# A hybrid decoder step: the beginning reordered, and column tiles in the modulation, the inverse and the sample z

## The chip, the core and the metric

The kernel runs as one program on one core of a Trainium2 chip. TensorE (matmuls, and beside them its weight loads), VectorE, ScalarE (ACT), GpSimd (POOL) and SyncE (SP, which issues the transfers) each work through their own instructions and wait for one another by semaphores. The metric is the time of one execution on the device in microseconds (us). All data are 32-bit floats. Most products split both operands into a high and a low part (`fp32r`) and add three products; the small ones are plain `f32` matmuls, which the profile shows as two instructions each.

## What is computed

One layer of a decoder: a modulated RMSNorm, one input projection, two groups of heads (a state-space one, SSD, and a gated delta rule, GDN), an output projection, a gate and a residual. It is applied to a prompt of 2048 rows and to 32 sample rows (8 sequences of 4). Cut to what matters here:

```python
mod = silu(c) @ w_ada + b_ada                     # c: 9 rows (1 prompt, 8 samples), w_ada: 1024 x 3072
shift, scale, gate = split(mod, 3)
h = rmsnorm(x, norm_w) * (1 + scale) + shift
proj = h @ w_in                                   # columns: z, conv inputs, gates of both head groups
xbc, _ = causal_conv4_silu(xbc_raw); qkv, _ = causal_conv4_silu(qkv_raw)
# GDN, per head and chunk:
A = strict_lower((beta * k) @ k.T * decay) + I
u, w = solve_triangular(A, [beta * v, beta * k * exp(gcum)])
# state passes from chunk to chunk; y = rmsnorm(o) * silu(z)
out = x + gate * (concat(ssd, gdn) @ w_out)
y = rmsnorm(out, final_norm_w)
```

## The kernel before

**Pieces.** The prompt is worked through in four pieces of 512 rows (`p` from 0 to 3). A piece holds its modulated rows transposed, as `hhi` and `hlo`: eight tiles k of 128 features by 512 rows. The last piece carries the 32 sample rows as 32 further columns. In a piece, the input projection runs through 104 half tiles of weights: a conv tile (128 output columns) has two halves of four k, twelve matmuls of 512 columns each; a z pair (256 output columns) has four quarters of two k. A half's weights come as 256 KB of floats into a buffer `xin` (three of them), and ACT and POOL split them into high and low (`want`, lines 495 and 496); some halves are stored split for later pieces. Four split halves can wait at once. Conv tiles add up in PSUM buffers of the tag `ip`, of which there are three; the smaller products use three of the tag `bk`. After its second half, a conv tile is evacuated by ACT and VectorE (`conv`, lines 536 to 549).

**Order.** TensorE's order is written out: each piece of work is entered with a time `tau` in units of about one conv half (`at(tau, f)`), and the work is issued by rising `tau`, 106 units to a piece. The order of the other engines and of SP's transfers is made by a planner that simulates the program; their waits follow from the data. `fill` enters weight halves into one list, by rising `tau`, so that `want` can load ahead.

**The beginning.** Ahead of the entered work, TensorE gets in this order: the first half of the shift (`ada_shift(0)`), the sums of squares of the first piece (`stat_first`), their spread over the partitions (`stat_row(0)`), the first half of the scale (`ada_scale(0)`). A half is 512 of the 1024 features. `ada_cols` makes 512 columns of the modulation: for each of eight k the nine columns of `sc` (silu of c) are the left side and 512 columns of `w_ada` are streamed past them (line 168), into nine rows of PSUM; ACT copies the nine rows (line 170), four transposes (line 173) turn them so that features are partitions, and VectorE adds the bias (line 174). The sums of squares use 32 matmuls with one streamed column each (line 300). `h_load` scales the x tiles by the row norm, `h_make` applies scale and shift and splits (lines 313 to 315). Only the first four k of `h` are made then; the other half (`second_half`) is entered at 2.3, after the first half of the first conv tile at 2. The gates (32 columns, `gates`) are made in five steps, entered at 0, 2.5, 4.1, 8.3 and 10.3: the product with the first four k, the product with the others, the turn (line 424) and the start of a chain on VectorE and ACT, the cumulative sum (lines 371 and 372), and the turn that is stored for the decays.

**The inverse.** For two heads at a time (a pair, 16 in the program) the eight 128 x 128 triangular matrices of a piece are inverted: blocks of 32 on VectorE, then `b2_1` to `b2_4` put the blocks together with matmuls. `b2_3` and `b2_4` (lines 852 to 864) are eight matmuls each, on 64 output rows and 64 streamed columns, evacuated in one copy each. Behind them come the `hop`s, which carry the state from chunk to chunk.

**Sample z.** In the last piece `z_pair` also makes z for the 32 sample rows: the rows are the left side (32 columns of `hhi` or `hlo`) and 256 columns of weights are streamed, three products per k (`zmm`, line 619).

**The gate columns** (`ada_gate`, line 195) are made among the last hops of the last piece, in two times four parts of two k, again with nine columns of `sc` on the left, and go to memory as rows. After that the pools are freed, and the output projection follows with the sample rows' heads among it.

## Time and profile before

| | |
|---|---|
| time, median of 3 runs | 2328.43 us (2324.95 to 2330.56) |
| profiled execution, its own time | 2327.78 us |
| its span in the profile | 2326.1 us |
| granted TensorE clock, mean | 0.979 |
| TensorE matmuls busy | 2200.8 us (95%) |
| TensorE weight loads busy | 1864.9 us (80%) |
| VectorE busy | 1481.9 us (64%) |
| ACT busy | 953.1 us (41%) |
| POOL busy | 826.7 us (36%) |
| read and written in memory | 289.89 MB, 95.30 MB |

A line such as `49.07 0.50 PE L414 MATMUL pbk<-hhi,wg 128*64 128x512 f32 x1 [3.98 <-ACT hhi L314]` is an instruction of TensorE (PE) at 49.07 us that took 0.50 us, made by line 414, which writes the PSUM tile `pbk` from `hhi` and `wg`: 128 rows by 64 columns of weights, 512 streamed columns; before it the engine was idle for 3.98 us until ACT had written `hhi`. "x8" puts eight like it together. PEld are weight loads, SPq is SyncE's issue of a transfer. Ends of matmuls are modelled, so that a start is a better mark than an end.

### The profile page before, as it was taken

Reading aid. Unit: us, or ns where it says so; the run is one execution under the profiler, and the core shown is the slowest. Engines: PE = TensorE matmul, PEld = TensorE weight load, DVE = VectorE, ACT = ScalarE, POOL = GpSimd, SP = SyncE. Lnnn points to the kernel's source line nnn. Section 1 sums busy time; section 2 is a strip of 40 time slices with the busy share of each in tenths; the row PEclk is TensorE's granted clock in tenths of the full one; section 3 lists DMA queues with packets and bytes.
Section 4 is the critical chain, followed back from the end, with each engine's and each line's share of the span. In section 5 each row is a group of like instructions: output and inputs, shape, how many; then the busy total and the mean of one; then the engine's idle time right before and its main releaser. Section 6 shows DMA issues by size and latency. Waiting matters only on the chain. (4 is left out here: it accounts for less than half of the span.)

```text
span 2326.1 us, 41856 instructions
## 1 busy us (share of the span) xinstructions
PE 2200.8 (95%) x15405; PEld 1864.9 (80%) x15405; DVE 1481.9 (64%) x3574; ACT 953.1 (41%) x2680; POOL 826.7 (36%) x1052
## 2 busy tenths in 40 slices
PE   6999999989999999999999989999999799998998
PEld 3688878868897887889788889998899377786786
DVE  2466868786767768675666776668676564454323
ACT  2534556454536445442533453435433432231111
POOL 3255665554437243411522241215211554322000
PEclk8999999999999999999999999999999999999999
DMA  6354655555766675465645544555445563643321
GB/s 239 113 167 152 191 166 180 181 181 174 225 214 209 213 225 183 143 193 165 191 153 179 178 135 132 180 154 157 150 147 160 165 211 125 191 155 128 129 86 52
DMA packets 241112, 387.94 MB, mean 167 GB/s; under 512 B 75880, under 2 KB 132968, under 8 KB 240908
## 3 DMA queue, kind: packets, MB, share of 16 engines
q1 hardware_dynamic: 240908, 385.28, 52.2%
q8 instruction: 121, 1.98, 0.3%
q14 instruction: 83, 0.68, 0.1%
HBM read 289.89 MB, written 95.30 MB: 166 GB/s over the span
## 5 line engine op out<-in xcount | busy, mean ns | idle before, releaser
L531 PE MATMUL pip<-hhi,w 128*128 128x512 f32 (+1 forms) x2880 | 823.7, 362 | 6.7 <-DVE kT L549 4.9
L531 PEld LDWEIGHTS pip<-hhi,w 128*128 128x128 f32 x2880 | 515.0, 190 | 85.0 <-issue 6.9
L531 PE MATMUL pip<-hlo,w 128*128 128x512 f32 (+1 forms) x1440 | 509.8, 354 | 0.0
L619 PE MATMUL pip<-w,hhi 128*128 128x256 f32 x2048 | 382.6, 287 | 0.3 <-DVE cv L549 0.3
L496 POOL TENSOR_TENSOR w<-xin,w 128x512 fp32r<-128x512 f32 x156 | 202.6, 1301 | 378.3 <-ACT w L495 344.8
L619 PEld LDWEIGHTS pip<-w,hhi 128*128 128x128 f32 x2048 | 316.5, 190 | 2.4 <-DVE cv L549 0.5
L531 PEld LDWEIGHTS pip<-hlo,w 128*128 128x128 f32 x1440 | 274.5, 191 | 36.9 <-issue 4.5
L619 PE MATMUL pip<-w,hlo 128*128 128x256 f32 x1024 | 289.4, 283 | 0.0
L1185 PE MATMUL pip<-wohi,mh 128*128 128x512 f32 x480 | 195.3, 407 | 7.4 <-ACT mh L1169 7.2
L619 PEld LDWEIGHTS pip<-w,hlo 128*128 128x128 f32 x1024 | 194.8, 190 | 0.0
L1185 PE MATMUL pip<-wohi,ml 128*128 128x512 f32 x480 | 189.7, 395 | 1.1 <-DVE ml L1176 1.0
L1185 PE MATMUL pip<-wolo,mh 128*128 128x512 f32 x480 | 189.1, 394 | 0.8 <-DVE wolo L238 0.8
L539 DVE SCALAR_TENSOR_TENSOR tr<-pip,cw,tr 128x509 f32<-128x509 f32 (+5 forms) x240 | 152.8, 637 | 40.2 <-ACT tr L536 37.1
L539 DVE SCALAR_TENSOR_TENSOR cv<-pip,cw,cv 128x509 f32<-128x509 f32 (+2 forms) x180 | 114.7, 637 | 44.6 <-ACT cv L536 42.5
L1000 POOL TENSOR_TENSOR L<-L,g_gc 128x512 f32<-128x512 f32 x64 | 70.9, 1120 | 198.4 <-DMA L<-rowsd 198.1
L495 ACT CAST w<-xin 128x512 fp32r<-128x512 f32 x156 | 95.1, 612 | 80.9 <-PE pip L619 25.9
L795 DVE TENSOR_TENSOR tl<-dl,ul 128x60 f32<-128x60 f32 (+21 forms) x432 | 121.0, 280 | 9.3
L797 DVE TENSOR_TENSOR dl<-dl,tl 128x60 f32<-128x60 f32 (+21 forms) x432 | 119.1, 276 | 9.0
L1185 PEld LDWEIGHTS pip<-wohi,mh 128*128 128x128 f32 x480 | 91.4, 190 | 27.0 <-ACT mh L1169 7.8
L1185 PEld LDWEIGHTS pip<-wohi,ml 128*128 128x128 f32 x480 | 91.0, 190 | 22.8 <-DVE ml L1176 3.0
L1185 PEld LDWEIGHTS pip<-wolo,mh 128*128 128x128 f32 x480 | 91.4, 190 | 18.2 <-DVE wolo L238 1.1
L1169 ACT CAST mh<-pch 128x512 fp32r<-128x512 f32 (+1 forms) x60 | 33.7, 562 | 166.4 <-PE pch L1166 166.3
(433 smaller groups left out, 4141.3 us busy)
## 6 DMA issues: line engine op xcount, KB each, us to landing
w<-wsp SPq DMA_DIRECT2D x260, 512.0 KB
wsp<-w SPq DMA_DIRECT2D x104, 512.0 KB
xin<-in_w_in SPq DMA_DIRECT2D x156, 256.0 KB
L<-rowsd SPq DMA_DIRECT2D x64, 256.0 KB
mx<-mixd SPq DMA_DIRECT2D x28, 512.0 KB
E<-rowsd SPq DMA_DIRECT2D x32, 256.0 KB
ul<-ud SPq DMA_DIRECT2D x64, 128.0 KB
mixd<-z SPq DMA_DIRECT2D x16, 512.0 KB
```

What stands on the lines that cost most here:

```text
L495: mark("ACT", s.copy(hi, rv))
L496: mark("POOL", g.tensor_tensor(lo, rv, hi, ALU.subtract))
L531: pe.matmul(pp, a[:, k, :], b[:, kk, cols], start=(i == 0), stop=(i == 23))
L539: v.scalar_tensor_tensor(u[:, c0 + dd:c0 + w], pp[:, 0:w - dd], cw[:, ci, k:k + 1], u[:, c0 + dd:c0 + w], ALU.mult, ALU.add)
L619: pe.matmul(out.rearrange("p (t c) -> p t c", t=2), a[:, k, cols], ws[b][:, :, k % 2, :], start=(first and k == 0 and e == 0), stop=(k == ...
L795: v.tensor_tensor(tmp[:, 0:r, 0:w], _bc(dl[:, 0:r, m], [P, r, w]), ul[:, m, m + 1:32].unsqueeze(1).to_broadcast([P, r, w]), ALU.mult)
L797: v.tensor_tensor(dl[:, 0:r, m + 1:32], dl[:, 0:r, m + 1:32], tmp[:, 0:r, 0:w], ALU.add)
L1000: g.tensor_tensor(L[:], L[:], _bc(G()["gc"][:, gi * 8 + q * 4:gi * 8 + q * 4 + 4, c], [P, 4, P]), ALU.subtract)
L1169: s.copy(mh[:, :, 0:n], ptv)
L1185: pe.matmul(pos[hb][0:m, :], a[:, k, 0:m], b[q * 4 + k][:, hb * 512:(hb + 1) * 512], start=(q == 0 and k == 0 and j == 0), stop=(q == 3 an ...
```

## The change

- **Modulation on column tiles.** The left side `sc` is widened to 32 columns (23 of them zero). The product of k goes to the 32 PSUM rows from 32 (k mod 4), so that k and k + 4 add up in one strip and there are four strips. ACT copies all 128 rows; four matmuls with `sel` (four unit matrices of 32 one above the other) turn the columns and add the strips in one. In `ada_gate` one matmul with `sel` adds the strips, after a copy by ACT into `pq`.
- **Statistics.** One matmul per k with a left side of ones and 512 streamed columns; VectorE picks the diagonal and sums it (two operations) to get the row sums by partition.
- **Order.** `stat_first` stands ahead of `ada_shift(0)`. All eight `h_load`s are entered ahead of the first `h_make`s. The second half of shift and scale stands at 0.9 and 1.1, and so do the other four `h_make`s.
- **Half tiles first.** In the first piece the first three conv tiles have their first halves at 1, 1.2 and 1.4 and their second halves at 5, 6 and 7. A conv tile's two halves are entered separately in the list of weights, everywhere. The gates' steps of the first piece stand at 0, 4.9, 6.4, 9 and 10.3.
- **The inverse.** In `b2_3` and `b2_4` the matmuls of chunks c and c + 4 alternate between the two halves of the output rows, and the results are evacuated in two copies each.
- **Sample z.** `hhi` gets 32 more columns, which hold the low part of the sample rows. One matmul per k takes hi and lo together (64 columns on the left) against the high weights, a second one takes hi against the low weights; at the end ACT copies the lower 32 rows and VectorE adds them.
- **Taps.** The conv taps and biases are loaded by themselves and halved where they lie; `ct` and `th9` move into rotating buffers, and `id2` is replaced by `sel`.

```diff
-    vec = const.tile([P, 220], F32, name="vec")
-    nc.sync.dma_start(vec[:], vecs)
+    vec = const.tile([P, 40], F32, name="vec")
+    nc.sync.dma_start(vec[:], vecs[:, 0:40])
...
+    cwb = const.tile([P, 5 * NT], F32, name="cwb")
+    nc.sync.dma_start(cwb[:], vecs[:, 40:220])
+    v.tensor_scalar(cwb[:], cwb[:], 0.5, None, ALU.mult)
...
+    ct = mk(trp, [P, T], "tr")[:, 0:KD * 9].rearrange("p (k c) -> p k c", c=9)
+    nc.sync.dma_start(ct, c_t)
...
+    sc = keep.tile([P, KD, 32], F32, name="sc")
+    g.memset(sc[:], 0.0)
...
+    sel = keep.tile([P, 32], F32, name="sel")
+    for q in range(0, P, 32):
+        v.tensor_copy(sel[q:q + 32], ident[q:q + 32, q:q + 32])
+
+    def ada_mm(pa, k, w):
+
+        q = 32 * (k % 4)
+        pe.matmul(pa[q:q + 32, :], sc[:, k, :], w, start=(k < 4), stop=(k >= 4))
...
-            pe.matmul(pa[0:9, :], sc[:, k, :], raw[:, k % 2, :], start=(k == 0), stop=(k == KD - 1))
-        rowt = mk(trp, [P, T], "tr")[0:9]
-        s.copy(rowt, pa[0:9, :])
+            ada_mm(pa, k, raw[:, k % 2, :])
+        rowt = mk(trp, [P, T], "tr")
+        s.copy(rowt[:], pa[:])
         pt = psum("o")
         for k in range(4):
-            pe.transpose(pt[:, k * 9:(k + 1) * 9], rowt[:, k * P:(k + 1) * P], ident[0:9, 0:9])
+            pe.matmul(pt[:, k * 9:(k + 1) * 9], rowt[:, k * P:(k + 1) * P], sel[:, 0:9], start=True, stop=True)
...
-                pe.matmul(pa[0][0:9, :], sc[:, k, :], raw[:], start=(k == 0), stop=(k == KD - 1))
+                ada_mm(pa[0], k, raw[:])
             if k0 == KD - 2:
+                pq = mk(trp, [P, T], "tr")
+                s.copy(pq[:], pa[0][:])
+                pa[0] = psum("ip")
+                pe.matmul(pa[0][0:32, :], sel[:], pq[:], start=True, stop=True)
...
-    hhi = hw.tile([P, KD, T + NS], F32R, name="hhi")
+    hhi = hw.tile([P, KD, T + 2 * NS], F32R, name="hhi")
...
-            for c in range(NC):
-                pe.matmul(pr[:, c:c + 1], sq_[:, c * P:(c + 1) * P], ones[:, 0:1], start=(k == 0 and c == 0),
-                          stop=(k == KD - 1), skip_group_check=True)
+            pe.matmul(pr[:], ones[:], sq_, start=(k == 0), stop=(k == KD - 1))
+
+        dg = mk(trp, [P, T], "tr")[:].rearrange("p (c t) -> p c t", c=NC)
+        v.tensor_tensor(dg, pr[:].rearrange("p (c t) -> p c t", c=NC), ident.unsqueeze(1).to_broadcast([P, NC, P]),
+                        ALU.mult)
...
+        v.tensor_reduce(stats[0][:], dg, axis=mybir.AxisListType.X, op=ALU.add)
...
+        v.tensor_copy(hhi[:, :, T + NS:T + 2 * NS], hlo[:, :, T:T + NS])
...
-    def conv_tile(tau, n, p, ci, hc, dst):
-
-        d = fill(tau, [(n, 0, False), (n, 1, False)])
+    def conv_tile(tau, n, p, ci, hc, dst, tau1=None):
+
+        d = {}
+        tau1 = tau + 1 if tau1 is None else tau1
+        ds = (fill(tau, [(n, 0, False)]), fill(tau1, [(n, 1, False)]))
...
                 for k in range(2 * j, 2 * j + 2):
-                    zmm(d["s"][0:NS, 0:256], k, slice(T, T + NS), ws, True)
+                    for m, b in ((2 * NS, 0), (NS, 1)):
+                        pe.matmul(sv[0:m], hhi[:, k, T:T + m], ws[b][:, :, k % 2, :], start=(k == 0 and b == 0),
+                                  stop=(k == KD - 1), skip_group_check=True)
...
+                    s.copy(zt_, d["s"][NS:2 * NS, 0:256])
+                    v.tensor_tensor(zt_, d["s"][0:NS, 0:256], zt_, ALU.add)
...
-            conv_tile(so + 2 * i, n, p, ci, hc, dst)
+            if p == 0 and pr == 0 and i < 3:
+
+                conv_tile(1 + 0.2 * i, n, p, ci, hc, dst, so + 3 + i)
+            else:
+                conv_tile(so + 2 * i, n, p, ci, hc, dst)
...
-            for c in range(8):
-                pe.matmul(pw[64:128, c * 64:(c + 1) * 64], U[:, c, 64:128], dt2[:, c, :], start=True, stop=True)
-            s.copy(p2x[64:128], pw[64:128, :].rearrange("p (c n) -> p c n", c=8))
+            for c in range(4):
+                cc = slice(c * 64, (c + 1) * 64)
+                for e in range(2):
+                    o = 64 * (1 - e)
+                    pe.matmul(pw[o:o + 64, cc], U[:, e * 4 + c, 64:128], dt2[:, e * 4 + c, :], start=True, stop=True)
+            for e in range(2):
+                o = 64 * (1 - e)
+                s.copy(p2x[64:128, e * 4:e * 4 + 4, :], pw[o:o + 64, 0:256].rearrange("p (c n) -> p c n", c=4))
...
-        for i, t in enumerate((0, 1, 2.9, 7.3, 9.3) if p else (0, 2.5, 4.1, 8.3, 10.3)):
+        for i, t in enumerate((0, 1, 2.9, 7.3, 9.3) if p else (0, 4.9, 6.4, 9, 10.3)):
...
-    at(2.3, second_half)
+    at(0.9, lambda: ada_shift(1))
+    at(1.1, lambda: ada_scale(1))
+    for k in range(4, KD):
+        at(1.1, lambda k=k: h_make(0, k))
...
+        stat_first()
         ada_shift(0)
-        stat_first()
...
         load_wg()
+        for k in range(KD):
+            h_load(0, k)
         for k in range(4):
-            h_load(0, k)
             h_make(0, k)
```

`b2_4` is changed like `b2_3`, with VectorE's copies in the place of ACT's.

More of the change, by code (lines that the diff above doesn't have):

```diff
@@ L87, in hymba_step_kernel @@
     mixw = vec[:, 24:40]
-    ct = const.tile([P, KD, 9], F32, name="ct")
-    nc.sync.dma_start(ct[:], c_t)
     rw = const.tile([P, 64], F32, name="rw")
@@ L202, in ada_gate @@
         return part
-    hhi = hw.tile([P, KD, T + NS], F32R, name="hhi")
+    hhi = hw.tile([P, KD, T + 2 * NS], F32R, name="hhi")
     hlo = hw.tile([P, KD, T + NS], F32R, name="hlo")
     wg2 = keep.tile([P, KD, 64], F32R, name="wg2")
-    id2 = keep.tile([64, 32], F32, name="id2")
-    for q in (0, 32):
-        v.tensor_copy(id2[q:q + 32], ident[q:q + 32, q:q + 32])
     halo = keep.tile([P, NT, 3], F32, name="halo")
@@ L423, in gates @@
         for c in range(NC):
-            pe.matmul(pt[:, c * 32:(c + 1) * 32], gr[:, c * P:(c + 1) * P], id2[:], start=True, stop=True)
+            pe.matmul(pt[:, c * 32:(c + 1) * 32], gr[:, c * P:(c + 1) * P], sel[0:64], start=True, stop=True)
         if p == SP:
-            pe.matmul(pt[0:NS, 128:160], grs, id2[:], start=True, stop=True)
+            pe.matmul(pt[0:NS, 128:160], grs, sel[0:64], start=True, stop=True)
         raw = mk(b1, [P, NC + 1, 32], "g_raw")
@@ L551, in q0 @@
         def q0():
-            want(d["i0"])
+            want(ds[0]["i0"])
             d["pp"] = pp = psum("ip")
@@ L581, in conv_tile @@
         at(tau, q0)
-        at(tau + 1, q1)
+        at(tau1, q1)
     def z_pair(tau, n, p, mcol, done):
@@ L861, in b2_4 @@
             pz = psum("bk")
-            for c in range(8):
-                pe.matmul(pz[0:64, c * 64:(c + 1) * 64], p2x[:, c, :], U[:, c, 64:128], start=True, stop=True)
-            v.tensor_copy(U[0:64, :, 64:128], pz[0:64, :].rearrange("p (c n) -> p c n", c=8))
+            for c in range(4):
+                cc = slice(c * 64, (c + 1) * 64)
+                for e in range(2):
+                    pe.matmul(pz[64 * e:64 * e + 64, cc], p2x[:, e * 4 + c, :], U[:, e * 4 + c, 64:128], start=True,
+                              stop=True)
+            for e in range(2):
+                v.tensor_copy(U[0:64, e * 4:e * 4 + 4, 64:128],
+                              pz[64 * e:64 * e + 64, 0:256].rearrange("p (c n) -> p c n", c=4))
         at(so + 31.7 + e, b2_0)
@@ L1011, in first @@
                 sct = mk(b2, [P, P], "sct")
-                s.copy(sct[:], psc[:, P:2 * P])
+                s.copy(sct, psc[:, P:2 * P])
                 px = psum("bk")
```

34 lines of the change are left out of this document (13 added, 21 removed).

## The prediction

> **What bounds the kernel now.** I read the page first, then the busy time by stage, then TensorE's instructions in order of time at the beginning, and last the groups by line for the parts that the change touches.
>
> ```profile
> span 2326.1 us, 41856 instructions
> PE 2200.8 (95%) x15405; PEld 1864.9 (80%) x15405; DVE 1481.9 (64%) x3574; ACT 953.1 (41%) x2680; POOL 826.7 (36%) x1052
> ```
> ```profile
> 0.00:80.00 80.00, 56.84 (x175) 24.92 (x176) 17.38 (x37) 22.93 (x39) 19.27 (x42) 0.83 0.51 183
> 130.00:1335.00 1205.00, 1164.66 (x8425) 1002.30 (x8425) 869.40 (x2062) 569.92 (x1576) 511.72 (x611) 0.99 0.59 185
> 1335.00:1850.00 515.00, 487.15 (x4395) 448.43 (x4392) 357.52 (x1054) 214.52 (x706) 145.74 (x185) 0.99 0.49 152
> ```
> The columns of the second view are span, PE, PEld, DVE, ACT, POOL, granted clock, DMA share and GB/s. From 130 to 1850 us TensorE is busy 1164.66 of 1205 and 487.15 of 515 us at a clock of 0.99: its instruction stream sets the end, and what is taken out of it comes off the time, less what falls into a wait (68 us idle in these 1720 us, 4%). The first 80 us are different: 23 us idle, and a clock of 0.83.
>
> TensorE at the beginning (start, length, operands, in brackets the idle time before):
>
> ```profile
> 12.09 1.88 PE L168 MATMUL pbk<-vs,sc 128*9 128x512 f32 x4
> ...
> 15.52 1.88 PE L168 MATMUL pbk<-kd,sc 128*9 128x512 f32 x4
> 18.84 0.41 PE L173 MATMUL po<-cs,tr 9*128 9x9 f32 x4 [1.45 <-ACT tr L170]
> ...
> 32.92 2.07 PE L283 MATMUL pbk<-E,ones 128*128 128x512 f32 x2 [2.47 <-DVE E L280]
> 44.67 0.41 PE L173 MATMUL po<-cs,tr 9*128 9x9 f32 x4 [0.67 <-ACT tr L170]
> 49.07 0.50 PE L414 MATMUL pbk<-hhi,wg 128*64 128x512 f32 x1 [3.98 <-ACT hhi L314]
> 52.80 0.40 PE L531 MATMUL pip<-hhi,w 128*128 128x512 f32 x1
> 55.68 1.89 PE L168 MATMUL pbk<-qd,sc 128*9 128x512 f32 x4
> ...
> 75.81 0.69 PE L414 MATMUL pbk<-hhi,wg 128*64 128x512 f32 x1 [3.98 <-ACT hhi L314]
> 79.59 0.61 PE L531 MATMUL pip<-hhi,w 128*128 128x512 f32 x1
> ```
> One f32 matmul is two instructions, so x4 is two k, and 12.09 to 15.52 are two such groups, 1.72 us each. A quarter of the modulation (8 k) takes 4 x 1.72 = 6.9 us, with nine of 128 columns in use; four quarters are 27.5 us. Only at 79.59 are both halves of h there, with one conv half (52.80 to 55.68) done.
>
> **The beginning.** The four modulation quarters go on four column tiles of 32. The program already has such a set:
>
> ```profile
> 2084.36 1.06 PE L1499 MATMUL po<-L,gr 128*32 128x512 f32 x8
> 2085.36 0.66 PE L1166 MATMUL pch<-cs,mx 128*128 128x128 f32 x4
> ```
> Four f32 matmuls, each with its own moving operand, end in 1.0 us, where L168 has two in 1.72. So 8 k are about 2.0 us if the data are there, plus the turn (here against the 9-row block of ones and zeros, which also adds the four strips): 0.67 to 1.45 idle behind ACT's copy and 0.41 for itself. Then the transfers decide, by the DMA view of the first 110 us:
>
> ```profile
> GB/s 67 102 321 401 388 388 383 386 384 385 390 385 397 281 86 296 12 0 0 0 0 183 103 0 0 0 0 0 0 0 0 101 248 48 124 254 96 271 130 105
> kT<-in_w_ada SPq DMA_DIRECT2D x3, 512.0 KB
> ```
> and SyncE's own queue of issues in order of time:
> ```profile
> 24.34 0.42 SPq L167 DMA_DIRECT2D vs<-in_w_ada  x1
> ...
> 40.97 17.18 SPq L494 DMA_DIRECT2D xin<-in_w_in  x2
> ```
> The GB/s row is in slices of 2.75 us: 2.45 MB by 11 us, then 0.386 MB per us. A quarter is 4 x 512 KB = 2.1 MB or 5.4 us, and the first 512 columns of x are as large. In the new order: small loads and x (2.46 MB) by 11.0, shift 0 by 16.4, scale 0 by 21.9, gate weights and two conv halves (0.65 MB) and shift 1 by 29.0, scale 1 by 34.4. Splitting the taps' load adds one issue of 0.4 us on SP before x, and the conditioning load moves behind it; both lie in the first 4 us, as does POOL's clearing of the 32-wide left side, and x's 5.4 us of transfer is what is waited for.
>
> Now TensorE: the statistics' 8 matmuls of 512 columns (0.86 each) follow x, end 13. Shift 0 ends at 17.6, its turn at 19.4. The ones row then 2.07 as at 32.92, ACT's copy 0.6, so at 22 VectorE can scale the eight x tiles; the same work before, from the timelines of VectorE and ACT:
>
> ```profile
> 35.65 5.84 DVE L309 TENSOR_TENSOR cv<-cv,sq 128x512 f32<-128x512 f32 x6 [2.78 <-ACT sq L285]
> 45.59 2.93 ACT L313 ACTIVATE cv<-cv,mod,s 128x512 f32<-128x512 f32 x4 [0.96 <-DVE s L183]
> ```
> Eight take 5.4 to 7 us. Scale 0 is there at 21.9 and turned at 24.7; from the old turn's end (45.08) to the first gate matmul (49.07) is 4.0 us, 3.5 of it from ACT's start at 45.59. If VectorE takes the eight first, ACT starts only at 29. First gate matmul: 28.7 to 32.5, I take 30. Then TensorE in its written order: gates 3.7 (49.07 to 52.80, half clock), shift 1 3.1, conv half 0 of the first tile 2.8, scale 1 3.1, conv half 0 of tiles two and three 5.6: 48.3. The second half of h is ready 4.0 us after scale 1's end of 42.7, at 46.7, so nothing waits; second gates 8 x 0.23 = 1.9: **50.2**. A conv half is 2.8 us from
>
> ```profile
> 93.08 0.39 PE L531 MATMUL pip<-hlo,w 128*128 128x512 f32 x1
> 93.78 0.40 PE L531 MATMUL pip<-hlo,w 128*128 128x512 f32 x1
> ```
> (0.70 per three, four times). At 79.59 the old order had done two halves fewer, so the gain is 79.6 + 5.6 - 50.2 = **35.0 us**.
>
> One wait is new. The gates' second step now stands at 6.4 and its third at 9 (4.1 and 8.3 before), which leaves two conv halves between them instead of four.
>
> ```profile
> 85.47 1.07 PE L424 MATMUL pbk<-id,sq 64*128 64x32 f32 x8
> 94.84 0.26 DVE L366 TENSOR_TENSOR g_ln<-g_sp,nega 128x96 f32<-128x96 f32 x1
> ```
> The chain from the turn's end to g_ln takes 95.1 - 86.5 = 8.6 us, and 5.6 us of TensorE work cover it: 3.0 us of wait, more (to 6) since three conv tiles now end 2.8 us apart and share VectorE with the chain. Queued behind the waiting matmul are the fourth tile's second half and the key and query turns. I take 4 us. Beginning: **-31** (38 if the chain is covered, 20 if a load comes late as below).
>
> **The inverse's last step.** Sixteen pairs, two sets of eight f32 matmuls of 64 columns each, now alternating between column halves. TensorE's timeline:
>
> ```profile
> 307.97 1.15 PE L856 MATMUL pbk<-dt,U 128*64 128x64 f32 x16
> ...
> 312.02 1.15 PE L863 MATMUL pbk<-U,p2x 128*64 128x64 f32 x16
> ...
> 316.39 1.02 PE L1030 MATMUL pbk<-hs,cv 128*128 128x512 f32 x2
> 317.35 1.15 PE L1035 MATMUL pbk<-xdt,L 128*64 128x64 f32 x32
> 318.43 0.50 PE L619 MATMUL pip<-w,hhi 128*128 128x256 f32 x2
> ```
> and of the evacuations, by the view of line 857 and by ACT's timeline:
> ```profile
> L857 ACT COPY p2x<-pbk x16: 581/583/585, 210.1 to 1802.5; 64x512 f32<-64x512 f32 x16
> 1844.31 0.37 ACT L903 COPY qd<-po 128x256 f32<-128x256 f32 x1 [0.64 <-PE po L898]
> ```
> L1035 alternates halves already: 32 instructions in the 1.15 us (1.08 to the next start) that L856 and L863 need for 16. Each set becomes 0.54, so 32 x 0.53 = 17 us. The evacuations become two of 256 columns (ACT 2 x 0.37 for 0.58, VectorE alike); they are covered by the 4 us between the two sets (307.97 to 312.02), and uncovered they would cost 0.2 x 32 = 6 us. The 4% of waits, with their chains beginning further back, take some: **-14.5** (-17 to -10).
>
> **Sample z.** In the last piece hi and lo stand beside each other, so two matmuls per k replace three.
>
> ```profile
> 1403.65 0.28 PE L619 MATMUL pip<-w,hlo 128*128 128x256 f32 x1
> 1403.77 0.40 PE L619 MATMUL pbk<-w,hhi 128*32 128x256 f32 x2
> ...
> 1404.47 0.60 PE L896 MATMUL pch<-vp,kd 128*128 128x128 f32 x4
> ```
> Six in 0.70 us, so 2 x 0.117 per step, 4 steps, 8 pairs: 7.5 us. The copy, the sum and one copy into hhi are small and behind the end of each pair. New is that 64 and 32 columns alternate. From 128 to 32 columns the rows show no gap; before L1035 there is 0.96 - 2 x 0.427, 0.1 us. At 0.1 per change, 16 x 8 changes are 12.8 us, so the bounds are -7.5 and +5.3; these matmuls have the form of the first rows (fp32r on 256 columns), and I take **-6.5**. The Trainium skill (TensorEngine Tiling (Array Packing), section Key Properties) says that changing the tiling mode drains TensorE, which speaks for the bad end; by it the sum below would be 12 us smaller. The rows around 1403.77 show no such drain between modes.
>
> **The gate columns at the end.** Eight parts of two k:
>
> ```profile
> 1802.41 1.88 PE L195 MATMUL pip<-xin,sc 128*9 128x512 f32 x4
> 1804.23 0.49 PE L1009 MATMUL pbk<-cv,cv 128*128 128x128 f32 x2
> 1832.31 0.71 PE L896 MATMUL pch<-vp,kd 128*128 128x128 f32 x4 [2.65 <-ACT vp L892]
> ```
> Two tiles overlap, 1.8 to 1.0 each: -6.4. Each of two columns gains a sum over the strips (0.86) behind a copy by ACT that TensorE waits for (about 1.1): +3.9. What is left fills waits like that at 1832: **-1** (-3 to +3). The taps scaled in place save one small VectorE operation in the first 5 us: 0.
>
> Sum: 31 + 14.5 + 6.5 + 1 = 53 us off the profiled execution's own 2327.8 us (1.7 beside its span; the median is 2328.4): **2275 us**.
>
> **Rivals.**
> *A load in the way* (beginning). SP issues in order. If the third conv half's load, which needs a buffer that the gate weights or the first half hold, is put ahead of scale 1's, that waits until about 33 and lands past 40 instead of 34.4; with the gates' chain at 6 the beginning gives 20: **2286**. For it: the row at 40.97, where two such loads held SP for 17 us. Against it: there all of L167's loads, as at 24.34, had been put ahead of them.
> *Nothing waits*: the gates' chain is covered and the 4% take nothing: 38 + 17 + 7.5 + 3 = 65.5, **2262**. Against it 8.6 against 5.6 us.
> *The strips do not overlap*, so the change does not do what it says: four quarters stay 27.5 us, the inverse 0, the gate columns +4. The new order alone lets the second gates end at about 59.5: 25.7 - 4 + 6.5 - 4 = 24, **2304**. L1499 and L1035 speak against it.
> *The inverse's second copy stands late* (slower). ACT works in order; if the second of the two copies of p2x stands behind other work, TensorE waits at the next set with all that is behind it. It costs the 16 pairs (wait x 16): beyond 53 / 16 = 3.3 us each the kernel is slower, at 4.5 it is 2327.8 - 53 + 72 = **2347**. Against it: L857's copy is 0.58 in all 16, with 4 us of room. The same page of the Trainium skill, section PSUM Bottleneck, says that tiling does not speed up PSUM's evacuation; no run here shows which copy would be late.
>
> **How the numbers follow.** Forecast 0.60, a load in the way 0.19, nothing waits 0.12, no overlap 0.04, the late copy 0.05. A measurement here tells 0.2% (4.7 us) from no change; of the late copy 0.02 lie within it. Faster 0.95, same 0.02, slower 0.03. The range from 2257 to 2297 holds the forecast's own (bounds of the beginning, of z and of the waits), the load in the way and most of the case without waits; outside are the last two and the tails, under 0.2.
>
> **What would show it.** Right: the first L414-like gate matmul near 30 us, the second gates' end near 50, a wait of 3 to 6 us at the gates' cumulative sum (L371 before), L856's sixteen in 0.54 us, four z sample matmuls in 0.47 us. Wrong: modulation groups of 6.9 us with data present, a gap at each change between 64 and 32 columns, or new idle time before the inverse's last set.

## The result, and the profile after

The changed kernel takes **2294.07 us** (median of 4 runs, 2292.64 to 2298.36) against 2328.9 for the kernel before: a ratio of 0.9856, 95% interval 0.9837 to 0.9874. It is 34 us faster, by 1.4%. The prediction was 2275 with a range of 2257 to 2297: the range holds the time, the likeliest value does not; 53 us were expected and 34 came. The profiled execution took 2294.92 us, its span is 2293.2.

The busy time on the page of the profile after, and then busy time by stage (columns as in the prediction: span, PE, PEld, DVE, ACT, POOL, granted clock, DMA share, GB/s):

```profile
PE 2154.2 (94%) x15313; PEld 1833.8 (80%) x15313; DVE 1492.9 (65%) x3601; ACT 959.6 (42%) x2706; POOL 821.3 (36%) x1053
```
```profile
0.00:75.00 75.00, 52.12 (x222) 28.42 (x222) 31.75 (x64) 34.16 (x59) 27.31 (x49) 0.92 0.64 228
130.00:1300.00 1170.00, 1121.23 (x8259) 965.27 (x8258) 857.98 (x2047) 562.18 (x1568) 502.73 (x605) 0.99 0.59 187
1300.00:1820.00 520.00, 486.18 (x4405) 447.06 (x4403) 366.40 (x1075) 223.36 (x735) 142.75 (x186) 0.97 0.49 152
```
TensorE's busy time fell by 2200.8 - 2154.2 = 46.6 us and the time by 33: some 14 us of what was taken out of its stream became idle time. From 130 us on it is busy 96% and 93% of the time at a clock of 0.99 and 0.97, so it still sets the end; the first 75 us have a clock of 0.92 and 23 us idle.

TensorE's timeline at the beginning, after (start, length, operands, in brackets the idle time before):

```profile
16.91 0.62 PE L167 MATMUL pbk<-kT,sc 128*32 128x512 f32 x2
...
18.53 0.60 PE L167 MATMUL pbk<-kd,sc 128*32 128x512 f32 x2
...
31.59 0.69 PE L430 MATMUL pbk<-hhi,wg 128*64 128x512 f32 x1 [5.26 <-ACT hhi L329]
...
36.91 1.07 PE L167 MATMUL pbk<-qd,sc 128*32 128x512 f32 x2
...
41.67 0.48 PE L549 MATMUL pip<-hhi,w 128*128 128x512 f32 x1
...
57.04 0.45 PE L430 MATMUL pbk<-hlo,wg 128*64 128x512 f32 x1 [1.02 <-DVE hlo L330]
57.33 0.39 PE L549 MATMUL pip<-hhi,w 128*128 128x512 f32 x1
...
63.96 0.50 PE L549 MATMUL pip<-hhi,w 128*128 128x512 f32 x1
...
76.74 0.71 PE L387 MATMUL pbk<-g_ln,cs 128*128 128x96 f32 x2 [6.28 <-DVE g_ln L382]
```
A modulation quarter is over in 1.7 us (16.91 to about 18.6) instead of 6.9: the four strips run side by side. The first gate matmul starts at 31.59 (forecast 30), the second gates are over at 57.33 (forecast 50.2), and the wait at the gates' cumulative sum is 6.28 us (forecast 3 to 6, taken as 4). In between, the second shift quarter with its turn lasts from 36.91 to 41.67, 4.8 us instead of 3.1: its first matmuls take 1.07 us where those of the first quarter take 0.62, at a granted clock of 0.50 from 31.5 to 36.5, after the idle time of 5.26.

Why the wait at 76.74 is so long is seen on VectorE (lines 368 to 382 are the gates' chain, 557 to 567 conv tiles):

```profile
70.80 0.20 DVE L370 TENSOR_SCALAR g_au<-g_w 128x96 f32<-128x96 f32 x1
71.93 0.69 DVE L567 SCALAR_TENSOR_TENSOR tr<-pip,tr 128x512 f32<-128x512 f32 x1 [0.93 <-ACT pip L566]
72.54 0.74 DVE L557 SCALAR_TENSOR_TENSOR kT<-pip,cwb,kT 128x511 f32<-128x511 f32 x1
73.20 0.69 DVE L371 TENSOR_TENSOR g_ln<-g_ln,g_au 128x96 f32<-128x96 f32 x1
```
The chain's step at 73.20 needs the one that was over at 71.0. Ahead of it stand two operations of conv tiles, and the first of them waits 0.93 us for ACT, which loads a table for it first:

```profile
70.00 1.28 ACT L566 ACT_TABLE_LOAD   x1
```
So 2.2 us pass between two steps that followed each other at once in the kernel before:

```profile
90.20 0.21 DVE L354 TENSOR_SCALAR g_au<-g_w 128x96 f32<-128x96 f32 x1
90.45 0.26 DVE L355 TENSOR_TENSOR g_ln<-g_ln,g_au 128x96 f32<-128x96 f32 x1
```
The whole chain, from the gates' turn (over at 63.96) to the cumulative sum, takes 12.8 us, where it took 8.6 before.

One set of the inverse, and the view of the second set's line for TensorE's matmuls (what they waited for, us and times):

```profile
286.25 0.69 PE L887 MATMUL pbk<-dt,U 128*64 128x64 f32 x16
286.87 0.50 PE L549 MATMUL pip<-hhi,w 128*128 128x512 f32 x1
```
```profile
L898 PE MATMUL pbk<-U,p2x x256: 222/222/270, 193.9 to 1768.2; 128*64 128x64 f32 x128
its engine sat idle before it (us, times) until:
  ACT p2x L890: 1.4, 2
```
From a set's start to the next instruction it is now 0.62 us instead of 1.08: 0.46 saved, where 0.53 was forecast. Two of the sixteen second sets wait for ACT's copy of p2x, which is now two instructions, 1.4 us together, and these two sets then take 1.0 us each. One of them:

```profile
290.57 1.07 PE L898 MATMUL pbk<-U,p2x 128*64 128x64 f32 x16 [0.66 <-ACT p2x L890]
```
Summed from the starts in the traces, the 32 sets take 20.54 us instead of 34.38: 13.8 us saved (forecast 17). In the kernel before, the matmuls of the second sets never wait for this copy.

Sample z in the last piece:

```profile
1376.27 0.63 PE L623 MATMUL pbk<-w,hhi 128*64 128x256 f32 x4
1376.73 0.61 PE L934 MATMUL pch<-vp,kd 128*128 128x128 f32 x4
```
Four matmuls that alternate between 64 and 32 columns are done in 0.46 us (forecast 0.47), where six took 0.70. Summed over the 32 such groups of the last piece it is 15.06 us instead of 21.84: 6.8 us saved.

One loss was not in the prediction. TensorE's and ACT's timelines in the second piece, after:

```profile
707.41 1.12 PE L1053 MATMUL pbk<-cs,cv 128*128 128x128 f32 x4 [4.35 <-ACT U L878]
```
```profile
701.94 0.63 ACT L993 ACTIVATE xsq<-st 128x512 bf16<-128x512 f32 x1 [4.69 <-DVE st L990]
...
706.25 0.63 ACT L275 ACTIVATE xsq<-xin 128x512 bf16<-128x512 f32 x1 [0.52 <-DMA xin<-in_x_p]
...
707.00 0.36 ACT L878 COPY U<-pbk 32x256 f32<-32x256 f32 x1
```
The same place in the kernel before (TensorE, and ACT):

```profile
728.11 0.60 PE L1015 MATMUL pbk<-cs,cv 128*128 128x128 f32 x4
```
```profile
726.69 0.37 ACT L850 COPY U<-pbk 32x256 f32<-32x256 f32 x1
...
729.09 0.63 ACT L955 ACTIVATE xsq<-st 128x512 bf16<-128x512 f32 x1 [1.64 <-DVE st L952]
```
ACT's copy into U frees the `bk` buffer that TensorE needs next. Before, it stood ahead of ACT's squares (of `st` and of the next piece's rows); now it stands behind them, and the squares wait for VectorE and for a transfer. TensorE waits 4.35 us, and its next instructions take twice their time (1.12 for 0.60). Nothing of the change is on these lines: the order of ACT is the planner's, and it came out differently.

To see where a kernel stands against the one before, the start of the same instruction is taken in both traces and subtracted. Six milestones will do: the first piece's cumulative sum of the gates (97.7 us before), a state update of the second piece ahead of the place above (707.1), a pair's key product behind it (747.0), the last piece's cumulative sum (1362.8), the output projection's first matmul (1859.5) and its last (2317.7). Positive is earlier than before, in us. It is one execution of each kernel, and executions of one kernel lie up to 16 us apart (e2: 2321.5 to 2337.7), so the columns are read for where a kernel gains or falls back, and small differences say little. Some traces are of an execution longer than the median of their kernel: e1's took 2324.55 us beside a median of 2320.17, e2's 2335.88 beside 2329.81, e9's 2294.22 beside 2290.20.

| kernel | 97.7 | 707.1 | 747.0 | 1362.8 | 1859.5 | 2317.7 | ratio of times, 95% |
|---|---|---|---|---|---|---|---|
| changed | 21.0 | 25.3 | 19.4 | 27.9 | 33.2 | 33.4 | 0.9856 (0.9837-0.9874) |
| e1 inverse alone | -2.5 | 1.4 | 2.0 | 3.9 | 4.5 | 3.5 | 0.9949 (0.9934-0.9964) |
| e2 sample z and taps | -0.5 | -6.3 | -12.3 | -12.0 | -8.1 | -7.9 | 0.9990 (0.9974-1.0005) |
| e3 beginning alone | 16.8 | 16.1 | 11.3 | 11.0 | 8.1 | 9.7 | 0.9941 (0.9926-0.9956) |
| e4 changed, squares held | 19.6 | 22.4 | 19.3 | 22.3 | 31.1 | 32.4 | 0.9857 (0.9836-0.9878) |
| e5 taps alone | 0.5 | -1.3 | -6.0 | -6.3 | -6.9 | -10.5 | 1.0021 (1.0006-1.0036) |
| e6 column tiles, old order | 15.1 | 13.2 | 13.2 | 10.1 | 9.0 | 8.3 | 0.9931 (0.9904-0.9957) |
| e7 new order, one strip | 2.4 | 4.2 | -3.4 | -4.8 | -6.5 | -5.5 | 1.0001 (0.9986-1.0017) |
| e8 changed, old gate columns | 18.4 | 24.8 | 19.4 | 24.0 | 28.6 | 31.3 | 0.9846 (0.9825-0.9867) |
| e9 changed, shift earlier | 24.7 | 27.2 | 22.6 | 27.1 | 31.6 | 33.5 | 0.9810 (0.9791-0.9829) |
| e10 e9 and gates moved | 23.0 | 29.4 | 24.7 | 28.8 | 32.6 | 36.2 | 0.9815 (0.9801-0.9830) |
| e11 columns, inverse, z | 14.7 | 10.5 | 11.4 | 16.8 | 24.6 | 27.3 | 0.9864 (0.9843-0.9886) |
| e12 changed, old inverse | 20.8 | 22.5 | 18.3 | 19.6 | 25.8 | 23.8 | 0.9905 (0.9885-0.9926) |

The ratios are each against runs of the kernel before beside them (its medians were 2331.8, 2332.0 and 2334.2 us in these sets), so the ratios are compared, not the times. Expectations that were written from 2328 us are 4 to 6 us low for these sets.

### The profile page after: what moved, and what is told of

It is laid out like the page before. It is cut to its first block, busy times and chain, and to the rows that moved or that the text cites. A ratio compares the mean times of both kernels' runs of the same rounds, so it can differ in the third digit from the quotient of the medians.

```text
span 2293.2 us, 41738 instructions
## 1 busy us (share of the span) xinstructions
PE 2154.2 (94%) x15313; PEld 1833.8 (80%) x15313; DVE 1492.9 (65%) x3601; ACT 959.6 (42%) x2706; POOL 821.3 (36%) x1053
## 5 line engine op out<-in xcount | busy, mean ns | idle before, releaser
L557 DVE SCALAR_TENSOR_TENSOR tr<-pip,cwb,tr 128x509 f32<-128x509 f32 (+5 forms) x240 | 152.8, 637 | 41.7 <-ACT tr L554 38.6
L557 DVE SCALAR_TENSOR_TENSOR cv<-pip,cwb,cv 128x509 f32<-128x509 f32 (+2 forms) x180 | 114.7, 637 | 38.8 <-ACT cv L554 36.3
L825 DVE TENSOR_TENSOR dl<-dl,tl 128x60 f32<-128x60 f32 (+21 forms) x432 | 125.3, 290 | 9.0
L1221 PEld LDWEIGHTS pip<-wohi,mh 128*128 128x128 f32 x480 | 91.9, 191 | 27.1 <-ACT mh L1205 7.9
L1221 PEld LDWEIGHTS pip<-wolo,mh 128*128 128x128 f32 x480 | 92.1, 192 | 18.3 <-DVE wolo L251 1.1
```

What stands on the lines that cost most here:

```text
L557: v.scalar_tensor_tensor(u[:, c0 + dd:c0 + w], pp[:, 0:w - dd], cw[:, ci, k:k + 1], u[:, c0 + dd:c0 + w], ALU.mult, ALU.add)
L825: v.tensor_tensor(dl[:, 0:r, m + 1:32], dl[:, 0:r, m + 1:32], tmp[:, 0:r, 0:w], ALU.add)
L1221: pe.matmul(pos[hb][0:m, :], a[:, k, 0:m], b[q * 4 + k][:, hb * 512:(hb + 1) * 512], start=(q == 0 and k == 0 and j == 0), stop=(q == 3 an ...
```

## The experiments

The theory after the two traces: each part of the change saves on TensorE about what was worked out, the beginning less; and what is lost beside that is lost where an edit lets the planner put ACT's and VectorE's work in another order. The rivals: one of the parts is itself worth far less than its sum (the inverse's split copies, the new order, sample z), or the gate columns at the end cost what is missing.

### e1: the inverse alone

```diff
-            for c in range(8):
-                pe.matmul(pw[64:128, c * 64:(c + 1) * 64], U[:, c, 64:128], dt2[:, c, :], start=True, stop=True)
-            s.copy(p2x[64:128], pw[64:128, :].rearrange("p (c n) -> p c n", c=8))
+            for c in range(4):
+                cc = slice(c * 64, (c + 1) * 64)
+                for e in range(2):
+                    o = 64 * (1 - e)
+                    pe.matmul(pw[o:o + 64, cc], U[:, e * 4 + c, 64:128], dt2[:, e * 4 + c, :], start=True, stop=True)
...
```


> The kernel before with the two inverse steps on column halves alone. Theory (the parts add up; each of the 32 sets saves 0.47 us as in the changed kernel's trace; the idle time of 4.4 us near 707 us in the changed kernel comes from a new order on ACT that the beginning brings): 2328 less 12 to 15, 2313 to 2316 us, and no new wait behind line 850's copy in the second piece. Rival (the inverse's extra copies bring that wait): 2319 to 2323 us, with 4 us or more of idle time before the state-space transposes of the second piece's second pair.

Measured: 0.9949, 11.7 us less than before (2320.17 beside 2331.82 us), against 14.5 forecast and within its bounds of 17 and 10. The time lies in the rival's range, but from 2328 us the ratio gives 2316, and the wait that the rival needs, behind the copy into U in the second piece, is not in the trace. The view of the second set's line in this kernel, the row of what its matmuls waited for:

```profile
  ACT p2x L862: 1.5, 2
```
The 32 sets take 20.47 us, 13.9 less than before; two waits for the split copy give back 1.5: 12.4 us, about what was measured. The planner's order kept the place at 707 to 747 us whole (1.4 to 2.0 in the table).

### e2: sample z, with the taps in place

The edit is the two blocks of the change for z and for the taps; z needs the room that the taps' edit frees.

```diff
+                    for m, b in ((2 * NS, 0), (NS, 1)):
+                        pe.matmul(sv[0:m], hhi[:, k, T:T + m], ws[b][:, :, k % 2, :], start=(k == 0 and b == 0),
+                                  stop=(k == KD - 1), skip_group_check=True)
...
+    cwb = const.tile([P, 5 * NT], F32, name="cwb")
+    nc.sync.dma_start(cwb[:], vecs[:, 40:220])
+    v.tensor_scalar(cwb[:], cwb[:], 0.5, None, ALU.mult)
```


> The kernel before with sample z in one left side, and the taps scaled in place, which makes the room for it. Theory (no cost at the change from 64 to 32 columns): 32 steps by 0.24 us, 7.5 us less, with waits 2320 to 2324 us. Rival (the change of tile width drains TensorE, 0.1 us each): 2328 to 2334 us.

Measured: 0.9990, no change that can be told. This was a miss: 7 us were expected, and the time lies in the rival's range. The rival's drain is not there, though: in this trace too the 32 groups take 15.05 us instead of 21.84. The table says that the saving is there and hidden: the kernel is 12 us late when the last piece begins, long before the first z of the samples (in an execution 6 us longer than the median), and regains 4 us by 1859.5. So something ahead of sample z costs, and the other edit is the taps'.

### e5: the taps alone

```diff
-    v.tensor_scalar(cw[:], vec[:, 40:184].rearrange("p (t k) -> p t k", k=4), 0.5, None, ALU.mult)
-    v.tensor_scalar(cb[:], vec[:, 184:220], 0.5, None, ALU.mult)
+    cwb = const.tile([P, 5 * NT], F32, name="cwb")
+    nc.sync.dma_start(cwb[:], vecs[:, 40:220])
+    v.tensor_scalar(cwb[:], cwb[:], 0.5, None, ALU.mult)
```


> The kernel before with nothing changed but the taps loaded and scaled in place (one VectorE operation less in the first 5 us, less room taken in SBUF; TensorE's written order untouched). By the prediction's price of the edit: 0, so 2329 to 2333 beside a kernel before at 2331.8. Theory tested: the order that the planner writes for ACT and VectorE changes with any edit, and this alone takes what sample z saved in the run before. Then this kernel is slower than before by 3 to 7 us (2334 to 2339), and TensorE shows new waits behind ACT or VectorE in the second to fifth pieces (from 187 us on, and at the state's matmuls near 737 us) although its own instructions are the same. If it comes out at 0, what took sample z's gain lies in the z edit itself.

Measured: 1.0021 (1.0006 to 1.0036), 4.9 us slower (1.4 to 8.4), within the 3 to 7 of the theory. TensorE has the same 15405 instructions as before, and the edit saves one small VectorE operation. The place is the one seen above (ACT's timeline, then TensorE's):

```profile
730.38 0.63 ACT L956 ACTIVATE xsq<-st 128x512 bf16<-128x512 f32 x1 [4.12 <-DVE st L953]
...
732.00 0.36 ACT L851 COPY U<-pbk 32x256 f32<-32x256 f32 x1
```
```profile
732.41 1.12 PE L1016 MATMUL pbk<-cs,cv 128*128 128x128 f32 x4 [2.85 <-ACT U L851]
```
Against the rows of before, the same copy into U has gone behind the same square, and TensorE waits 2.85 us where it waited for nothing. Between 707.1 and 747.0 this kernel falls back by 4.7 us, the changed one by 5.9, e3 by 4.8, e7 by 7.6; e1, e6 and e11 do not. e3, e7 and the changed kernel all hold the taps' edit, but so do e6 and e11, which do not fall back. So the edit does not cause the stall by what it does; it is one of those by which the planner's order tips over. What in the planner tips it was not looked into. How much of the 4.9 us this one place makes isn't shown either. Over the runs of the set the granted clock is 0.9762 in the mean, for the kernel before 0.9775; as an estimate, if TensorE is busy all the time, 0.0013 of 2332 us is 3 us, so much of the loss can be half clock behind waits, here and elsewhere.

By difference, sample z is worth 0.9990 - 1.0021 = -0.31%, 7.2 us (some 5 either way, from both intervals), against 6.5 forecast. The table has 4.5 for it: between 1362.8 and 1859.5 e2 gains 3.9 us and e5 loses 0.6.

### e4: ACT's squares held back

The changed kernel, with ACT's squares (those of `st`, shown, and those of the next piece's rows) held behind the last weight cast in the written order.

```diff
-        s.activation(jk, y, AF.Square, accum_out=ss)
+        with hold("ACT"):
+            s.activation(jk, y, AF.Square, accum_out=ss)
```


> The changed kernel with ACT's squares (of the state-space output and of the row sums for the next piece) issued only behind the last weight cast entered before them. Theory (the wait before the state-space transposes near 707 us is one of ACT's order): that wait falls from 4.4 to under 2 us and the time to 2287 to 2291 us. Rival (TensorE is merely early there and would wait in any order): 2293 to 2296 us.

Measured: 0.9857, the same as the changed kernel. The time is the rival's, but the wait is not: TensorE waits 0.81 us at this place, as the theory had it (under 2). The hold did not take the square out of the way, though. One of `st` still stands ahead of the copy into U:

```profile
705.69 0.63 ACT L995 ACTIVATE xsq<-st 128x512 bf16<-128x512 f32 x1 [5.31 <-DVE st L991]
...
708.75 0.36 ACT L879 COPY U<-pbk 32x256 f32<-32x256 f32 x1
```
TensorE only comes later to it: it has waited 3.62 us some 12 us ahead, where the changed kernel waits 2.49. The fall between 707.1 and 747.0 shrinks from 5.9 to 3.1 us, and the kernel is behind the changed one elsewhere (22.3 against 27.9 at 1362.8). So no run here puts the order right, and what the stall at 707 costs in the end is not shown.

### e3, e6 and e7: the beginning, and its two halves

e3 has the change without its parts for the inverse, sample z and the gate columns; e6 the column tiles in the old order, e7 the new order with all modulation matmuls in one strip. All three have the taps in place; e6 has the old statistics, too, and e7 is without the inverse, sample z and the gate columns like e3. The strip of e7:

```diff
-        q = 32 * (k % 4)
-        pe.matmul(pa[q:q + 32, :], sc[:, k, :], w, start=(k < 4), stop=(k >= 4))
+        pe.matmul(pa[0:32, :], sc[:, k, :], w, start=(k == 0), stop=(k == KD - 1))
```
e6 keeps the new `ada_mm`, and the order of the kernel before, of which these lines are a part:

```diff
-        for i, t in enumerate((0, 1, 2.9, 7.3, 9.3) if p else (0, 4.9, 6.4, 9, 10.3)):
+        for i, t in enumerate((0, 1, 2.9, 7.3, 9.3) if p else (0, 2.5, 4.1, 8.3, 10.3)):
...
-    at(0.9, lambda: ada_shift(1))
-    at(1.1, lambda: ada_scale(1))
+    at(2.3, second_half)
```


> The kernel before with the beginning alone (column tiles, order, half tiles first, taps); inverse, sample z and gate columns as before. Theory: 21 us are gained by the gates' cumulative sum, and the new order on ACT takes some 3 to 7 back in the second piece: 2310 to 2315 us. Rival (nothing is lost later, the wait at 707 us belongs to the inverse): 2306 to 2308 us.

> The kernel before with the modulation on four column tiles (shift and scale, both halves of h), in the old order of the beginning; the new order of halves and the gates' new places are left out. Each quarter of the modulation then takes about 2 us on TensorE where its data are there, instead of 6.9. The transfers stay as they were, so the beginning's second half (modulation 55.7 to 75.8 before) should shorten by 8 to 12 us and the first by 2 to 4: 2318 to 2324 less what is lost later. Beginning with both parts ran 2318: if column tiles alone reach that, the new order brought nothing.

> The kernel before with the new order of the beginning and the gates' new places, and the modulation's matmuls all in one strip of 32 columns, one after another (the column tiles do not overlap). By the prediction's rival without overlap the second gates end at about 59.5 if all else is as forecast; with what was measured beside the forecast in the changed kernel (first gates at half clock, conv halves later) 64 to 70, against 77 to 80 before: 2315 to 2325.

Measured: e3 0.9941 (13.8 us), e6 0.9931 (16 us), e7 1.0001 (nothing). The column tiles in the old order bring as much as the whole beginning, within the intervals; the new order without them brings nothing that can be told. All three hold the taps' edit: against e5, the taps alone, e7 is 0.20% or 4.7 us faster (some 5 either way). By their times e6 (2319.45) is where it was expected, e7 (2332.85) and e3 (2317.96) are above; e3's ratio, from 2328, gives 2314, within its range. TensorE in e7:

```profile
15.93 1.90 PE L166 MATMUL pbk<-kT,sc 128*32 128x512 f32 x4
...
21.10 1.88 PE L166 MATMUL pbk<-kd,sc 128*32 128x512 f32 x4
...
75.68 0.45 PE L424 MATMUL pbk<-hlo,wg 128*64 128x512 f32 x1 [1.01 <-DVE hlo L325]
...
95.33 0.74 PE L381 MATMUL pbk<-g_ln,cs 128*128 128x96 f32 x2 [6.21 <-DVE g_ln L376]
```
and the cumulative sum in e6:

```profile
82.65 0.36 PE L380 MATMUL pbk<-g_ln,cs 128*128 128x96 f32 x2
```
With one strip a quarter is 6.9 us again, so it is the strips and not the wider left side that gain. The new order does bring forward the second gates (e7: 76.0 instead of 79.6, with two conv halves, 5.6 us, more behind it: 9.2 us), but 6.2 us go into the wait at the cumulative sum, which e6, with the gates at their old places, does not have at all. 2.4 us are left at 97.7, and the place at 707 takes those.

### e8: the old gate columns

```diff
-                ada_mm(pa[0], k, raw[:])
+                pe.matmul(pa[0][0:9, :], sc[:, k, 0:9], raw[:], start=(k == 0), stop=(k == KD - 1))
```
and without the copy to `pq` and the sum over the strips.

> The changed kernel with the gate columns of the end as before (nine columns, no sum over the strips, no copy behind which TensorE waits). The prediction had the new form at -1. Theory from the trace of the changed kernel: it costs about 4 us between 1770 and 1830 us (waits of 0.71, 0.68 and 3.53, 2.40, 1.48), so this one is at 2289 to 2291 beside a changed kernel at 2294; the waits at the sum over the strips are gone. Rival: the waits in that stretch move to the next step of the same chain, 2293 to 2296.

Measured: 0.9846 (0.9825 to 0.9867), not to be told from the changed kernel (the difference is 2 us, some 6.5 either way). My reading that the new waits at the sum over the strips cost 4 us fell: with the old form the stretch from 1362.8 to 1859.5 gains 4.6 us in the table, with the new one 5.3.

### e9 and e10: filling the idle time of the beginning

```diff
-    at(0.9, lambda: ada_shift(1))
+    at(-0.5, lambda: ada_shift(1))
```
and, in e10 only:

```diff
-        for i, t in enumerate((0, 1, 2.9, 7.3, 9.3) if p else (0, 4.9, 6.4, 9, 10.3)):
+        for i, t in enumerate((0, 1, 2.9, 7.3, 9.3) if p else (0, 4.9, 5.4, 9.95, 10.3)):
```


> The changed kernel with the second shift quarter of the modulation placed ahead of the first gates' matmuls instead of behind them. In the changed kernel TensorE stands idle for 5.26 us from the scale's turn (26.3) to the first gate matmul (31.59), and runs at half clock afterwards until 39 us; the quarter's data land at about 28. Theory: the quarter (4.8 us at half clock) moves into the idle time, the idle time falls to some 2 us, the granted clock stays up and the first gates take about 4 us instead of 5.3: the second gates' end goes from 57.3 to 50 to 53, the whole to 2287 to 2290 beside a changed kernel at 2294. Rival: the turn's copy on ACT comes late (it stands between the h tiles), TensorE waits for it ahead of the gates, and the second gates' end stays at 56 to 58: 2293 to 2296.

> As the run before, and the gates' second step 1 unit earlier and their third 0.95 later in the written order of TensorE (first piece only), so that more conv halves stand between them. The changed kernel waits 6.28 us at the gates' cumulative sum; the prediction had 4. Theory: this wait falls to 0 to 2 us and 3 to 5 us come off the time of the run before: 2283 to 2287. Rival: the chain behind the gates' turn is lengthened by the conv tiles' own VectorE work (they come sooner), and the wait falls by under 2 us: no better than the run before.

Measured: e9 0.9810 (0.9791 to 0.9829), e10 0.9815 (0.9801 to 0.9830). Both are below the changed kernel's 0.9856 and their intervals lie under its own (0.9837 at the low end); they were not run beside it. By ratio that is 10 us, by the times themselves (2290.20 and 2291.06 beside 2294.07) 3 to 4, and e9's profiled execution is no faster than the changed kernel's at the last milestone (33.5 beside 33.4). TensorE in e9:

```profile
29.25 1.05 PE L167 MATMUL pbk<-U,sc 128*32 128x512 f32 x4 [0.31 <-DMA U<-in_w_ada]
32.02 1.68 PE L185 MATMUL po<-sel,tr 128*128 128x9 f32 x8 [1.72 <-ACT tr L182]
...
53.31 0.45 PE L430 MATMUL pbk<-hlo,wg 128*64 128x512 f32 x1 [1.00 <-DVE hlo L330]
...
72.99 0.71 PE L387 MATMUL pbk<-g_ln,cs 128*128 128x96 f32 x2 [6.29 <-DVE g_ln L382]
```
The quarter runs as its data land, in the idle time. The copy of its strips on ACT comes between h tiles, as the rival had it, and TensorE waits 1.72 us for it; still the second gates end at 53.6 instead of 57.3. That the clock stays up was wrong; the same kernel by stretches (columns as above) has 0.58 here:

```profile
31.50:36.50 5.00, 4.48 (x15) 2.91 (x15) 4.32 (x5) 3.08 (x6) 2.96 (x2) 0.58 0.98 342
```
In e10 the wait at the cumulative sum is gone:

```profile
67.10 0.50 PE L549 MATMUL pip<-hhi,w 128*128 128x512 f32 x1 [2.94 <-DVE kT L567]
74.76 0.36 PE L387 MATMUL pbk<-g_ln,cs 128*128 128x96 f32 x2
```
In its place TensorE waits 2.94 us for VectorE to free a conv tile's buffer, so about half of the 6.3 is gained (e10 is 2.2 us ahead of e9 at 707.1), and the two kernels' times cannot be told apart: the theory had the wait right (0 to 2 us) and the gain wrong (3 to 5), the rival (the wait falls by under 2) had the gain right and the wait wrong. By ratio and by time e9 and e10 are the fastest kernels here; by how much is open.

### e11 and e12: the change without one part

e11 is the changed kernel with the old order and gate places (e6's lines) and the old gate columns; e12 with the old inverse:

```diff
-            for c in range(4):
-                cc = slice(c * 64, (c + 1) * 64)
-                for e in range(2):
-                    pe.matmul(pz[64 * e:64 * e + 64, cc], p2x[:, e * 4 + c, :], U[:, e * 4 + c, 64:128], start=True,
-                              stop=True)
...
+            for c in range(8):
+                pe.matmul(pz[0:64, c * 64:(c + 1) * 64], p2x[:, c, :], U[:, c, 64:128], start=True, stop=True)
```


> The changed kernel without the new order of the beginning and the gates' new places (both as before), and with the gate columns of the end as before: column tiles, inverse and sample z alone. By the runs so far column tiles gave -12.5 us in the old order, both together -13.9 and the new order alone 0: if the new order is worth nothing beside column tiles, this one is at 2292 to 2298, like the changed kernel. By the prediction the new order carried about two thirds of the beginning's 31 us: then 2304 to 2312.

> The changed kernel with the inverse's last step as before (sets of sixteen in 1.08 us instead of 0.54). The prediction had the edit at -14.5, alone on the kernel before it measured -11.7. Theory: each of 32 sets costs 0.47 again and this kernel is 10 to 15 us slower than the changed one, 2304 to 2309. Rival: in the changed kernel the planner's order of ACT takes more of it, under 8 us: 2299 to 2302.

Measured: e11 0.9864 (0.9843 to 0.9886), the same as the changed kernel within the intervals: beside column tiles, inverse and z, the new order with the gate columns is worth 0.08%, 2 us (some 6.5 either way), which is not told from nothing, nor from the 6.3 us by which the changed kernel leads e11 at 97.7. (The time, 2302.92, lies outside the expected 2292 to 2298; the ratio, from 2328.9, gives 2297.) e12 0.9905: without the new inverse 0.49% or 11.4 us are missing (some 6.5 either way), about the 11.7 that it brought alone. So the inverse adds up, as far as the intervals can tell; what does not add up is the rest.

## Why the prediction was right and where it was wrong

**The strips overlap** (the base of the change): right. 1.7 us for a quarter with its data there, 6.9 in one strip (e7). The row of L1499 in the kernel before had shown it.

**The beginning, -31: wrong by 10.** The lead at the cumulative sum is 21.0 us, near the lower bound of 20; but the late load for which that bound stood did not come: that the lead lies inside the bounds is in part luck. 7.1 of the 10 are lost by the second gates' end (57.33 against 50.2): 1.6 in the first gate matmul's start, 1.6 in the first gates (31.59 to 36.91, 5.3 us for 3.7), 1.7 in the second shift quarter, 0.6 in the scale and the halves, 1.6 in the second gates (3.5 us, with the wait of 1.02 for `hlo` among them). The step that failed is "Then TensorE in its written order": it let the half clock behind the idle time end with the first gates, and took hlo as ready with hhi. The late start of the first gate matmul has its own step, the statistics: they end at 16.9 instead of 13, because TensorE, busy without a gap from 7.70, takes 1.84 and 1.70 us for the first two pairs of instructions where 0.86 was put for each; the scale's turn is then over at 26.3 instead of 24.7. Of the other 2.9, 2.3 are the chain behind the gates: 6.28 us of wait for the 4 that I chose from bounds of 3 and 6. Another 0.4 is a wait for VectorE at 67.40. That the chain shares VectorE with conv tiles was named; its 12.8 us for 8.6 was not sized.

**And the credit was given to the wrong half.** The rival without overlap gave the new order 21.7 of the beginning's us by itself (25.7 - 4, from a second gates' end at 59.5). e7 is that case: 76.0. Its quarters of 6.9 us follow one another on the path: 57.3 + 4 x 5.2 = 78 would have been near it. e7's lead at 97.7 is 2.4 us, e6's 15.1: the strips give most of what the beginning gives, and the order takes back in the chain's wait most of what it brings forward.

**The inverse, -14.5: right**, a little high: 0.46 a set instead of 0.53 (13.8 us in all instead of 17), and 1.4 us of waits for the split copy. Measured -11.7 and -11.4. The copies "covered by the 4 us between the two sets" are covered in 14 of 16 pairs (the 4 us run from start to start, so the room was 3); the late-copy rival's mechanism is there in two pairs, at 0.7 us of wait and 0.4 of a slower set each, not at 3.3 in all sixteen.

**Sample z, -6.5: right.** 0.46 us for four, 6.8 us over the 32 groups in the trace; by difference of the runs 7.2, some 5 either way. The rows show no gap where 64 and 32 columns alternate; the rule of the Trainium skill weighed there (TensorEngine Tiling (Array Packing), section Key Properties) costs nothing that this trace can show.

**Gate columns, -1: not contradicted.** e8 can't tell it from nothing.

**Taps, 0: wrong, +4.9** (e5). The operations do cost nothing. What failed is the step that prices an edit by its own instructions: with a planner between the code and ACT's order, an edit also draws a new order, and this one holds a stall (2.85 us in e5, 4.35 in the changed kernel) with half clock about it.

Sum of the terms as measured: 21 (beginning at the cumulative sum) + 11.7 + 7.2 - 4.9 = 35, beside 34 measured. So of the 19 us that were missing, the beginning has about 10, the taps 5 and the inverse 3. This is not a proof: the 21 is from a single execution, the other terms are known to some 3.5 to 5 us each, so that they fit to 1 us is in part luck, and e3's lead of 16.8 does not all arrive at the end (13.8 by ratio, 9.7 in the table).

**"A load in the way"** gave 2286, nearer to the result, but for another reason: no load was late. In the changed kernel SyncE issued the last load of the second scale quarter ahead of the third conv half's, and TensorE started on that quarter at 44.64 without a wait. In e9's rows the last of the second shift's data are there at 29.25, forecast 29.0. SyncE's queue in the changed kernel:

```profile
26.61 0.37 SPq L179 DMA_DIRECT2D kd<-in_w_ada  x1
27.97 6.40 SPq L510 DMA_DIRECT2D xin<-in_w_in  x2
```

## What to carry to other kernels

Matmuls of few columns that stream long operands gain nearly their factor from column tiles (6.9 to 1.7 us for eight k at full clock), in the old order as in the new one; a new order of the work earns only what the chain behind it can follow. Where a planner orders the other engines, price an edit at its instructions and, beside them, at what a new order may cost: here 5 us for an edit that should cost nothing. Terms under that size can't be checked one by one by the whole time; the leads by milestone show where an order came out badly, and a sum over all instances of a group in the trace shows what the group itself saved. When a view lists waits, ask it for one engine: a weight load and its matmul that wait for the same copy are listed as two waits (six for the copy of p2x in the changed kernel, of which two are the matmuls'). Look at each stretch of idle time ahead of a busy one for the clock as well as for itself.

## What the hardware showed that was not expected

The way back to full clock was not of one length. e3, e8 and the changed kernel have the same instructions on TensorE in the beginning and the same idle time of 5.3 us ahead of the first gates. The changed kernel, e8 and e3 by stretches, those in which the clock came back (the second number is TensorE's busy time, the third from the end the granted clock):

```profile
36.50:41.50 5.00, 4.28 (x24) 1.34 (x23) 0.00 (x0) 1.72 (x3) 1.47 (x2) 0.71 0.76 279
41.50:46.50 5.00, 5.00 (x31) 2.74 (x30) 0.20 (x1) 0.62 (x1) 2.11 (x2) 1.00 0.22 79
```
```profile
41.50:46.50 5.00, 5.00 (x18) 4.28 (x19) 0.20 (x1) 0.19 (x1) 1.27 (x1) 0.57 0.26 91
```
```profile
46.50:51.50 5.00, 4.29 (x22) 1.58 (x21) 0.00 (x0) 1.20 (x2) 1.28 (x1) 0.73 0.00 0
```
In each of them the granted clock is 0.50 from 31.5 us up to the stretch with the number between, and 1.00 behind it. Taken as either half or full, it came back at about 39.4, 45.8 and 49.2 us (0.71 is 2.9 of the five us at half and 2.1 at full), so 8 to 18 us after the work began again at 31.6, with TensorE busy 77% to 100% of each five us. That accounts for the difference of these three kernels at 97.7 us: half clock for 6.4 us (e8) and 9.8 us (e3) longer costs at most 3.2 and 4.9, and they are 2.6 and 4.2 behind the changed kernel.

The Trainium skill (TensorE: Matmul & The Clock Gate, section The HAM clock gate) gives about 3.4 us of sustained work for the return, by which, as an estimate, it would be at 35 us; counted so, these three executions don't agree with it. But the work wasn't without gaps: TensorE waited 0.3, 0.6 and 0.7 us at about 34.6, 36.3 and 41. From the end of the last wait ahead of the return it is 3.1 us in the changed kernel, 4.5 in e8 and 7.8 in e3. So short waits can be part of the reason, but e3 stayed at half clock through 7.8 us without one. Why, and whether the same kernel would do it differently in another execution, no run here shows.
